# Two-layer hybrid encoder step: stage buffers laid out from both ends of on-chip memory, the last pair of each output projection reordered

## Chip, cores and metric

One core of one Trainium2 chip runs the whole kernel in one launch. The metric is device time in microseconds (us), the median of the runs. The engines are named as the profile names them: PE is TensorE's matmul and PEld its weight load, DVE is VectorE, ACT is ScalarE, POOL is GpSimd, SP is SyncE, which only issues transfers here. All operands are fp32; a matmul with fp32 precision is made of three passes over values that are split into a high and a low part.

## What is computed

A step of an encoder of two layers, width 2048, over 640 tokens (512 of a prompt, 128 of eight short samples). In each layer:

```python
h = rms_norm(x, norm_g)
z = h @ w_in                      # 2048 -> 4864 columns, in 38 blocks of 128
# a: GLU -> causal conv, width 31 -> LayerNorm -> swish -> pointwise product
# b: sliding-window attention, 16 heads;  c: attention into 256 memory rows, 4 heads
y = concatenate([y_a, y_b, y_c], -1) @ w_out   # each times its own SiLU gate
x = x + y
```

A final `rms_norm` follows the second layer. The keys, values and convolution tails are outputs as well.

## The kernel before, in words

**Layout.** Everything is kept transposed: features on the 128 partitions, the 640 tokens along the free axis. `R` holds 16 blocks of 128 features (first the residual stream x, then the attention outputs), and `HL` holds the same 16 blocks split into a high part (slots 0 to 15) and a low part (slots 16 to 31), which is what PE reads. A matmul of this kernel takes a 128x128 piece of a split weight and 320 tokens (half of them).

**Stages.** Each layer has an input stage and an output stage.

- The input stage (the loop over `ZT`, from line 907) makes one `proj` (line 737) for each of the 38 column blocks: four weight tiles of 128x512, each loaded by SP (`load`, line 147), split by ACT into `wh` (line 136) and by DVE into `wl` (line 137), and read by 24 matmuls (line 746). `wprep` (line 163) does the load and the split, out of three buffers each (`wr`, `wh`, `wl`). Convolution, attention and gates run beside it on the other engines and in between on PE.
- The output stage begins at line 1034. All 16 blocks of `R` are split into `HL` (line 1036). Output blocks j = 0 and j = 1 are plain projections with `proj` and `s_prep` (line 770), whose weights go through the buffers `sr` (raw, six of 128x768), `sh` and `sl` (two each). Beside them `combos` (line 780) forms sums and differences of the blocks of `R` and splits them into the tiles `th`/`tl` (`T[2]` to `T[4]`, 128x960 a piece, six pieces) and into `HL` itself (`T[1]`).
- The other output blocks are made two at a time by `s_pair` (line 815), a Strassen-like scheme with 7 products for 8 on 12 of the 16 input blocks. Its parts are: the product `p1` (18 matmuls); `plain` (line 835): the weights `a12` with half A of the tokens, the changed `a12` with half B (18 each), then the four other input blocks `KS` for j1 and for j2 (24 each); and the four `mixed` products `p7`, `p6`, `p4`, `p5` (18 each) with `T[3]`, `T[2]`, `T[4]`, `T[1]`. `plain` comes first; only the last pair of the second layer (`early`) has the mixed ones first.
- In the first layer all 16 output blocks are made this way; behind the last pair the next layer's `x_split` (line 877) rewrites `HL` from `R` and the first `proj` of the next input stage begins. In the second layer the pairs end at block 13; blocks 14 and 15 are made by the tail (from line 1058), which loads and splits eight weight tiles (`t_prep`), brings six blocks of the second token half back from DRAM (`y12d`, written at line 1038) and splits them into `HL`, and multiplies first 384, then 256 tokens (line 1096). The final norm and the output transfers follow.

**Buffers.** Buffers of a stage are drawn from groups that share one region of on-chip memory, one stage after the other. `phase_pools` (line 75) closes all open groups and opens the next ones from the low end: `wp` and `at` (input stage: `wr`, `wh`, `wl`, `rstd`; `at` holds what attention and convolution need), then `tt` and `sw` (output stage: the `th`/`tl` tiles; `sr`, `sh`, `sl`), then `wp` and `at` again (line 874), and at the end `tw` (line 1058: `y12`, `xr`, `xh`, `xl`). By the shapes, a partition of `wp` holds 20.5 KB, `tt` 45 KB, `sw` 30 KB and `tw` 45.5 KB. A new buffer waits for the old ones that lay in its place (`reuse_waits="tile"`).

**Order of the work.** A planner puts the instructions of each engine into one fixed order before the run, by their order in the program, with the weight preparations (`tc.high_priority`) preferred, and by a simulated timeline. All weight loads are issued by SP in program order (`load` chains them). On the chip each engine works through its list; transfers of `R`, `x1d`, `y12` and the like are issued by POOL.

## Time and profile before

| what | us |
| --- | --- |
| median of 3 runs (1858.0 to 1860.16) | 1858.42 |
| time of the profiled execution itself | 1861.93 |
| its span, first to last instruction | 1860.1 |
| PE busy | 1825.3 |
| DVE busy | 1258.2 |
| ACT busy | 789.3 |

The sums of the prediction are made in the profiled execution, whose own time is 1.83 us over its span and 3.51 us over the median. In the timeline rows below, a row gives the start in us, the busy time of the merged group, the engine, the line, the operation with the output and input tiles, and the count; in brackets stands the idle time of the engine just before and what ended it. PE's busy times contain a modelled end, so its matmuls overlap in them; distances between starts are the safer measure.

### The profile page before, as it was taken

Reading aid. Unit: us, or ns where it says so; the run is one execution under the profiler, and the core shown is the slowest. Engines: PE = TensorE matmul, PEld = TensorE weight load, DVE = VectorE, ACT = ScalarE, POOL = GpSimd, SP = SyncE. Lnnn points to the kernel's source line nnn. Section 1 sums busy time; section 2 is a strip of 40 time slices with the busy share of each in tenths; the row PEclk is TensorE's granted clock in tenths of the full one; section 3 lists DMA queues with packets and bytes.
Section 4 is the critical chain, followed back from the end, with each engine's and each line's share of the span. In section 5 each row is a group of like instructions: output and inputs, shape, how many; then the busy total and the mean of one; then the engine's idle time right before and its main releaser. Section 6 shows DMA issues by size and latency. Waiting matters only on the chain.

```text
span 1860.1 us, 32336 instructions
## 1 busy us (share of the span) xinstructions
PE 1825.3 (98%) x12612; PEld 1772.8 (95%) x12612; DVE 1258.2 (68%) x2562; ACT 789.3 (42%) x1609; POOL 160.8 (9%) x351
## 2 busy tenths in 40 slices
PE   8999999999999999999999999999999999999997
PEld 8999999999998999999999999999999999899996
DVE  7959988567555445966686999756755434776665
ACT  7831224557553334533352222555654333533331
POOL 1121110000000011100030000000000010110000
PEclk9999999999999999999999999999999999999998
DMA  8844442222222343533332332222232243452224
GB/s 280 296 116 107 104 128 76 69 65 72 87 81 74 92 154 118 186 117 114 111 108 71 81 88 79 77 66 72 65 89 81 75 131 130 128 188 75 83 79 139
DMA packets 89001, 202.30 MB, mean 109 GB/s; under 512 B 11872, under 2 KB 16912, under 8 KB 88816
## 3 DMA queue, kind: packets, MB, share of 16 engines
q1 hardware_dynamic: 68848, 139.75, 25.2%
q0 software_dynamic: 17536, 57.60, 10.0%
q10 hardware_dynamic: 2464, 2.88, 0.4%
q8 instruction: 99, 1.62, 0.4%
q14 instruction: 54, 0.44, 0.1%
HBM read 184.84 MB, written 20.33 MB: 110 GB/s over the span
## 4 chain that ended last, share of the span: by engine, by line
PE 95%; DVE 2%; DMA 1%; issue 0%; ACT 0%; DVEq 0%; ACTq 0%; POOLq 0%
PE z L746 60%; PE a L807 9%; PE z L807 8%; PE a L276 3%; PE z L299 2%; PE a L494 2%; PE a L537 2%; PE a L474 2%; PE z L1096 1%; DVE R L1129 1%; PE a L525 1%; DMA wr<-w_in 1%; PE a L633 1%; PE a L672 1%; PE a L659 1%; PE a L568 1%
## 5 line engine op out<-in xcount | busy, mean ns | idle before, releaser
L746 PE MATMUL z<-HL,wh 128*128 128x320 f32 x4864 | 950.4, 312 | 1.4 <-ACT wh L136 1.4
L746 PEld LDWEIGHTS z<-HL,wh 128*128 128x128 f32 x4864 | 768.4, 188 | 10.5 <-issue 5.7
L746 PE MATMUL z<-HL,wl 128*128 128x320 f32 x2432 | 570.4, 312 | 2.7 <-DVE wl L137 2.7
L746 PEld LDWEIGHTS z<-HL,wl 128*128 128x128 f32 x2432 | 409.4, 188 | 6.5 <-DVE wl L137 3.3
L136 ACT ACTIVATE wh<-wr 128x512 fp32r<-128x512 f32 x308 | 193.9, 630 | 472.1 <-PE z L746 384.5
L137 DVE TENSOR_TENSOR wl<-wr,wh 128x512 fp32r<-128x512 f32 x308 | 212.2, 690 | 184.6 <-ACT wh L136 172.2
L422 DVE SCALAR_TENSOR_TENSOR R<-R,sm 128x128 f32<-128x128 f32 (+1 forms) x480 | 235.3, 551 | 0.1
L136 ACT ACTIVATE sh<-sr 128x768 fp32r<-128x768 f32 (+1 forms) x133 | 103.4, 780 | 221.0 <-PE z L807 92.0
L807 PE MATMUL z<-HL,sh 128*128 128x320 f32 x728 | 160.7, 309 | 0.5 <-ACT sh L136 0.5
L137 DVE TENSOR_TENSOR sl<-sr,sh 128x768 fp32r<-128x768 f32 (+1 forms) x133 | 115.6, 871 | 41.6 <-ACT sh L136 41.6
L807 PEld LDWEIGHTS z<-HL,sh 128*128 128x128 f32 x728 | 121.7, 188 | 0.8 <-ACT sh L136 0.8
L807 PE MATMUL z<-HL,sl 128*128 128x320 f32 x364 | 113.8, 313 | 0.6 <-DVE sl L137 0.4
L807 PE MATMUL a<-th,sl 128*128 128x320 f32 x234 | 72.4, 309 | 0.8 <-DVE sl L137 0.8
L807 PE MATMUL a<-th,sh 128*128 128x320 f32 x234 | 72.3, 309 | 0.0
L807 PE MATMUL a<-tl,sh 128*128 128x320 f32 x234 | 72.3, 309 | 0.0
L807 PEld LDWEIGHTS z<-HL,sl 128*128 128x128 f32 x364 | 68.4, 188 | 3.0 <-DVE sl L137 2.9
L807 PE MATMUL a<-HL,sh 128*128 128x320 f32 x312 | 68.9, 309 | 0.0
L137 DVE TENSOR_TENSOR g<-a,g 128x512 fp32r<-128x512 f32 x80 | 49.6, 634 | 27.1 <-ACT g L136 26.5
L498 DVE CUSTOM_DVE_ANT_0 g<-a,R 128x256 f32<-128x256 f32 (+1 forms) x128 | 46.4, 388 | 23.4 <-PE a L494 20.0
L136 ACT ACTIVATE g<-a 128x512 fp32r<-128x512 f32 x80 | 42.3, 553 | 42.2 <-PE a L528 29.8
L510 ACT ACTIVATE g<-g,sml 128x256 f32<-128x256 f32 (+1 forms) x128 | 60.0, 472 | 0.0
L517 ACT ACTIVATE g<-g,sml 128x256 f32<-128x256 f32 (+1 forms) x128 | 51.5, 474 | 3.9 <-DVE sml L513 3.9
(262 smaller groups left out, 2579.0 us busy)
## 6 DMA issues: line engine op xcount, KB each, us to landing
wr<-w_in SPq DMA_DIRECT2D x304, 256.0 KB, 2.7
sr<-w_out SPq DMA_DIRECT2D x52, 384.0 KB, 3.2
sr<-w_out SPq DMA_DIRECT2D x42, 256.0 KB, 2.6
u<-w_mv SPq DMA_DIRECT2D x16, 512.0 KB, 3.5
u<-cmkT POOLq DMA_DIRECT2D x16, 512.0 KB, 4.2
u<-cmv POOLq DMA_DIRECT2D x16, 512.0 KB, 4.6
u<-w_mk SPq DMA_DIRECT2D x14, 512.0 KB, 4.3
R<-xT SPq DMA_DIRECT2D x16, 320.0 KB, 4.0
```

Of the source, the lines that this page charges most:

```text
L136: a = ac.activation(hi, raw, AF.Copy)
L137: v = ve.tensor_tensor(out=lo, in0=raw, in1=hi.bitcast(F32), op=ALU.subtract)
L276: pe.matmul(ps[ct][:, :256], w[:, ws], mslot(l, k, lo), start=k == 0 and n == 0, stop=k == NK - 1 and n == 2,)
L299: pe.matmul(psv[:, m, :], mslot(l, k, lo)[:, ms], w, start=k == 0 and n == 0, stop=k == NK - 1 and n == 2,)
L422: ve.scalar_tensor_tensor(out=o, in0=x, scalar=w, in1=o, op0=ALU.mult, op1=ALU.add)
L474: pe.matmul(ps[:, :HT], w[:, ws], x[:, k, :], start=n == 0, stop=n == 11)
L494: pe.matmul(ps[:, j, c0:256], q[:, p * P:(p + 1) * P], kk[n][h][:, (p - 1) * P + c0:(p + 1) * P], start=n == 0, stop=n == 1,)
L498: ve.tensor_tensor_reduce(out=x[:, j, c0:], in0=ps[:, j, c0:], in1=bt[:, c0:], scale=1.0, scalar=-3.0e38, op0=ALU.add, op1=ALU.max, accum_ ...
L510: ac.activation(x, x, AF.Exp, bias=ng[:, p:p + 1], accum_out=sm_[:, p:p + 1])
L517: ac.activation(x, x, AF.Copy, scale=rd[:, p:p + 1])
L746: pe.matmul(ps[:, s, :HT], w[:, ws], HL[:, lo * NK + k, s * HT:(s + 1) * HT], start=k == 0 and n == 0, stop=k == NK - 1 and n == 2,)
L807: pe.matmul(out, a[:, k * P:(k + 1) * P], b[:, k, :], start=start and k == 0 and i == 0, stop=stop and k == n - 1 and i == 2, skip_group_c ...
```

## The change

`phase_pools` is replaced by `open_pool` and `close_pool`, which open a group from the left or the right end and close one at a time. `wp` lies at the right end and `at` at the left. At the end of the input stage `at` is closed and `sw` takes its place at the left; `wp` stays open until output block j = 0, which now uses `wprep` with `wr`, `wh`, `wl`, has been written, and only then `tt` takes its place at the right. The last pair of each layer (before: of the second only) takes its mixed products first. In it the two `KS` weights are loaded ahead, then `turn(0)` closes `tt` and opens the next group at the right (`wp` in the first layer, `tw` in the second, with the read of `y12`), the `KS` products of j1 and j2 follow, then `turn(1)` (second layer: two tail weights, the split of `y12`), the result of j2, the `a12` products, `turn(2)` (the six other tail weights), and the result of j1. `sw` is closed behind that and `at` opened in its place. `xr` has two buffers where it had three.

```diff
--- before.py
+++ after.py
@@ -68,15 +68,17 @@
     dr = pool("dr", bass.MemoryType.DRAM)
 
     uid, last, cur = [0], {}, {}
-    phase = ctx.enter_context(ExitStack())
+    held_pools = {}
     home = {t: "wp" for t in ("wr", "wh", "wl", "rstd")}
     home |= {t: "at" for t in ("g2", "qh", "u5", "kc", "kh", "kl", "mh", "ml", "vh", "vl", "cqs")}
 
-    def phase_pools(*names):
-        phase.close()
-        for n in names:
-            uid[0] += 1
-            cur[n] = phase.enter_context(tc.tile_pool(name=f"{n}{uid[0]}", bufs=1, reuse_waits="tile"))
+    def open_pool(n, side):
+        uid[0] += 1
+        held_pools[n] = tc.tile_pool(name=f"{n}{uid[0]}", bufs=1, reuse_waits="tile", side=side)
+        cur[n] = held_pools[n].__enter__()
+
+    def close_pool(n):
+        held_pools.pop(n).__exit__(None, None, None)
 
     def tl(shape, tag, bufs, dt=F32, pl=None):
         uid[0] += 1
@@ -309,7 +311,8 @@
             gp.dma_start(mvd[l].rearrange("h p m d -> p h m d")[:, :, m, :], o)
 
     mraw = []
-    phase_pools("wp", "at")
+    open_pool("wp", "right")
+    open_pool("at", "left")
 
     def load_mem(j):
         if j:
@@ -812,7 +815,7 @@
     def add_to(out, ps):
         ve.tensor_tensor(out=out, in0=ps, in1=out, op=ALU.add)
 
-    def s_pair(l, j1, T, resid, early):
+    def s_pair(l, j1, T, resid, early=None):
         j2 = j1 + 1
         wj = [A["w_out"][l, j1], A["w_out"][l, j2]]
         cut = [slice(ks.start * P, ks.stop * P) for ks in (KA, KB, KS)]
@@ -832,24 +835,25 @@
         s_mm(X, p1, hl(KA, TA), True, True)
         add_to(R[:, j1, TA], X)
 
-        def plain():
-            z = pz()
+        z1 = z2 = None
+
+        def rest(z, j, start, raw=None):
+            with tc.high_priority():
+                w = s_split(raw or s_load(wj[j - j1][:, cut[2]]))
+            for s, cs in enumerate((TA, TB)):
+                s_mm(z[:, s, :HT], w, hl(KS, cs), start, True)
+
+        def plain(start):
             with tc.high_priority():
                 w = s_split(a12)
-            s_mm(z[:, 0, :HT], w, hl(KB, TA), True, False)
+            s_mm(z1[:, 0, :HT], w, hl(KB, TA), start, not start)
             with tc.high_priority():
                 sub(a12, a12, s2)
                 w = s_split(a12)
-            s_mm(z[:, 1, :HT], w, hl(KB, TB), True, False)
-            w = s_prep(wj[0][:, cut[2]])
-            for s, cs in enumerate((TA, TB)):
-                s_mm(z[:, s, :HT], w, hl(KS, cs), False, True)
-            add_to(half(R[:, j1, :]), z[:, :, :HT])
-            z = pz()
-            w = s_prep(wj[1][:, cut[2]])
-            for s, cs in enumerate((TA, TB)):
-                s_mm(z[:, s, :HT], w, hl(KS, cs), True, True)
-            add_to(half(R[:, j2, :]), z[:, :, :HT])
+            s_mm(z1[:, 1, :HT], w, hl(KB, TB), start, not start)
+
+        def into(j, z):
+            add_to(half(R[:, j, :]), z[:, :, :HT])
 
         def mixed(raw, n, out, start, dst):
             with tc.high_priority():
@@ -862,16 +866,36 @@
         p7 = (a21, 3, Dd, True, [(j2, TB)])
         p5 = (s1, 1, X, False, [(j2, TB), (j1, TB)])
         p4 = (a22, 4, Dd, False, [(j2, TA)])
-        if not early:
-            plain()
-        for a in (p7, p6, p4, p5):
-            mixed(*a)
+        order = (p7, p6, p4, p5)
         if early:
-            plain()
+            for a in order:
+                mixed(*a)
+            with tc.high_priority():
+                st = [s_load(w[:, cut[2]]) for w in wj]
+            early(0)
+            z1, z2 = pz(), pz()
+            rest(z1, j1, True, st[0])
+            rest(z2, j2, True, st[1])
+            early(1)
+            into(j2, z2)
+            plain(False)
+            early(2)
+            into(j1, z1)
+        else:
+            z1 = pz()
+            plain(True)
+            rest(z1, j1, False)
+            into(j1, z1)
+            z2 = pz()
+            rest(z2, j2, True)
+            into(j2, z2)
+            for a in order:
+                mixed(*a)
 
     for l in range(L):
         if l:
-            phase_pools("wp", "at")
+            close_pool("sw")
+            open_pool("at", "left")
         cur["rstd"] = rstd = tl([P, TOK], "rstd", 1)
         for k in range(0 if l else 8, NK):
             x_split(l, k)
@@ -1031,7 +1055,8 @@
                     push(samples.pop(0))
             step(7 if bg and bg[0] is not lnt else 2)
 
-        phase_pools("tt", "sw")
+        close_pool("at")
+        open_pool("sw", "left")
         for k in range(NK):
             split(R[:, k, :], None, HL[:, k, :], HL[:, NK + k, :])
         if l == L - 1:
@@ -1039,15 +1064,49 @@
         acc = w25()
         resid = A["xT"] if l == 0 else x1d
         done = NK if l == 0 else NK - 2
-        T = None
+        T, W = None, []
+
+        def t_prep(src):
+            with tc.high_priority():
+                raw = tl([P, 512], "xr", 2, F32, cur["tw"])
+                load(raw, src)
+                hi = tl([P, 512], "xh", 8, F32R, cur["tw"])
+                lo = tl([P, 512], "xl", 8, F32R, cur["tw"])
+                split(raw, None, hi, lo)
+                return hi, lo
+
+        def turn(step):
+            if step == 0:
+                close_pool("tt")
+                open_pool("tw" if l == L - 1 else "wp", "right")
+            if l < L - 1:
+                return
+            if step == 0:
+                cur["y12"] = tl([P, 6, HT], "y12", 1, F32, cur["tw"])
+                with tc.high_priority():
+                    gp.dma_start(cur["y12"], y12d)
+                return
+            for p in (range(2), range(2, 8))[step - 1]:
+                W.append(t_prep(A["w_out"][l, NK - 2 + p // 4][:, p % 4 * 512:(p % 4 + 1) * 512]))
+            if step == 1:
+                b12 = hl(KA, TB)
+                for g in (0, 3):
+                    ks = slice(g, g + 3)
+                    split(cur["y12"][:, ks, :], None, b12[0][:, ks, :], b12[1][:, ks, :])
+
         for j in list(range(2)) + list(range(2, done, 2)):
             if j < 2:
                 res = zt()
                 gp.dma_start(res, resid[j])
-                ps = proj([A["w_out"][l, j][:, c * 512:(c + 1) * 512] for c in range(4)], s_prep)
+                ps = proj(
+                    [A["w_out"][l, j][:, c * 512:(c + 1) * 512] for c in range(4)], s_prep if j else wprep
+                )
                 ve.tensor_tensor(out=half(R[:, j, :]), in0=ps[:, :, :HT], in1=half(res), op=ALU.add)
             else:
-                s_pair(l, j, T, resid, l == L - 1 and j + 2 == done)
+                s_pair(l, j, T, resid, turn if j + 2 == done else None)
+            if j == 0:
+                close_pool("wp")
+                open_pool("tt", "right")
             if j == 1:
                 T = combos()
             for i in range(j, j + 1 if j < 2 else j + 2):
@@ -1055,27 +1114,6 @@
                     gp.dma_start(x1d[i], R[:, i, :])
                 add_sq(i, i == 0, acc)
 
-    phase_pools("tw")
-
-    def t_prep(src):
-        with tc.high_priority():
-            raw = tl([P, 512], "xr", 3, F32, cur["tw"])
-            load(raw, src)
-            hi = tl([P, 512], "xh", 8, F32R, cur["tw"])
-            lo = tl([P, 512], "xl", 8, F32R, cur["tw"])
-            split(raw, None, hi, lo)
-            return hi, lo
-
-    y12 = tl([P, 6, HT], "y12", 1, F32, cur["tw"])
-    with tc.high_priority():
-        gp.dma_start(y12, y12d)
-        b12 = hl(KA, TB)
-        for g in (0, 3):
-            ks = slice(g, g + 3)
-            split(y12[:, ks, :], None, b12[0][:, ks, :], b12[1][:, ks, :])
-    W = [
-        t_prep(A["w_out"][L - 1, NK - 2 + p // 4][:, p % 4 * 512:(p % 4 + 1) * 512]) for p in range(8)
-    ]
     res = [zt(), zt()]
     for j in range(2):
         gp.dma_start(res[j], x1d[NK - 2 + j])
@@ -1134,6 +1172,8 @@
                 (sy if k % 4 == 1 else ac).dma_start(
                     A["yT"][k - 1:k + 1, :, cs].rearrange("k p n -> p k n"), R[:, k - 1:k + 1, cs]
                 )
+    close_pool("tw")
+    close_pool("sw")
 
 
 _OUT = {
```

## Rows read from the trace of the kernel before

**Rows 1.** What PE waited for over the whole span: engine, line, tile, the releaser, then us in total, times, longest us. 12 such rows make up 24.4 us; one of them.

```profile
PE z L1096 <- ACT xh L136: 2.3, 1, 2.3
```

**Rows 2.** The chain of waits, merged: start us, us, engine, tile, line, count. A stretch of the second layer's input stage and the last stretch of its last pair, both without a gap.

```profile
1120.44 30.07 PE z L746 x205
...
1796.63 12.33 PE z L807 x84
```

**Rows 3.** Timeline around the end of the first layer's input stage and the first weights of its output stage.

```profile
746.64 51.02 SPq L147 DMA_DIRECT2D sr<-w_out  x16
...
752.38 0.46 PE L746 MATMUL z<-HL,wl 128*128 128x320 f32 x2
...
753.26 1.14 ACT L136 ACTIVATE sh<-sr 128x512 fp32r<-128x512 f32 x2
...
753.93 0.86 PE L746 MATMUL z<-HL,sh 128*128 128x320 f32 x4 [1.10 <-ACT sh L136]
...
755.71 0.56 PE L746 MATMUL z<-HL,sl 128*128 128x320 f32 x2 [0.92 <-DVE sl L137]
```

**Rows 4.** The same place of the second layer.

```profile
1618.43 0.46 PE L746 MATMUL z<-HL,wl 128*128 128x320 f32 x2
...
1619.98 0.86 PE L746 MATMUL z<-HL,sh 128*128 128x320 f32 x4 [1.10 <-ACT sh L136]
...
1621.76 0.56 PE L746 MATMUL z<-HL,sl 128*128 128x320 f32 x2 [0.92 <-DVE sl L137]
```

**Rows 5.** Timeline 20 us later in the second layer, at the second weight tile of output block j = 1.

```profile
1632.41 2.23 DVE L775 TENSOR_TENSOR R<-R 128x960 f32<-128x960 f32 x2 [2.77 <-DMA y12d<-R]
...
1638.89 0.75 PE L746 MATMUL z<-HL,sh 128*128 128x320 f32 x4
...
1641.22 0.69 DVE L137 TENSOR_TENSOR sl<-sr,sh 128x512 fp32r<-128x512 f32 x1
...
1641.97 0.90 PE L746 MATMUL z<-HL,sl 128*128 128x320 f32 x2 [2.33 <-DVE sl L137]
...
1645.24 0.45 PE L746 MATMUL z<-HL,sl 128*128 128x320 f32 x2
```

**Rows 6.** Timeline of the turn from the first layer's last pair to the second layer's first projection (weights issued at 959.76).

```profile
959.76 34.72 SPq L147 DMA_DIRECT2D wr<-w_in  x12
...
962.85 3.00 ACT L139 ACTIVATE HL<-R,sm 128x640 fp32r<-128x640 f32 x4 [2.38 <-PE a L807]
...
964.70 0.31 PE L807 MATMUL a<-HL,sl 128*128 128x320 f32 x1
...
965.75 1.66 ACT L136 ACTIVATE wh<-wr 128x512 fp32r<-128x512 f32 x3
...
966.42 0.86 PE L746 MATMUL z<-HL,wh 128*128 128x320 f32 x4 [1.41 <-ACT wh L136]
...
968.44 0.56 PE L746 MATMUL z<-HL,wl 128*128 128x320 f32 x2 [1.16 <-DVE wl L137]
...
973.02 0.75 PE L746 MATMUL z<-HL,wh 128*128 128x320 f32 x4
```

**Rows 7.** Timeline of the turn from the second layer's last pair to the tail.

```profile
1791.23 26.31 SPq L147 DMA_DIRECT2D xr<-w_out  x8
...
1808.64 0.31 PE L807 MATMUL z<-HL,sl 128*128 128x320 f32 x1
...
1809.90 0.74 ACT L252 ACTIVATE w<-R 128x640 f32<-128x640 f32 x1 [2.83 <-DVE R L813]
1810.54 1.14 ACT L136 ACTIVATE xh<-xr 128x512 fp32r<-128x512 f32 x2
...
1811.21 0.62 PE L1096 MATMUL z<-HL,xh 128*128 128x384 f32 x2 [2.26 <-ACT xh L136]
...
1812.15 0.52 PE L1096 MATMUL z<-HL,xl 128*128 128x384 f32 x1 [0.32 <-DVE xl L137]
...
1815.90 0.34 PE L1096 MATMUL z<-HL,xl 128*128 128x384 f32 x1
```

**Rows 8.** Stretches of the span: us, then PE, PEld, DVE, ACT and POOL busy us (instructions), the granted TensorE clock as a share of full speed, DMA share, GB/s.

```profile
768.00:795.00 27.00, 26.85 (x184) 26.59 (x183) 20.96 (x26) 11.68 (x15) 7.47 (x14) 1.00 0.70 239
...
1640.00:1661.00 21.00, 18.07 (x110) 17.55 (x111) 19.51 (x23) 8.98 (x12) 6.39 (x12) 0.92 0.65 219
```

**Rows 9.** DVE's groups by shape, in 753 to 800 us and in 940 to 990 us: busy us, mean ns of one, idle before.

```profile
L137 DVE TENSOR_TENSOR tl<-R,th 128x960 fp32r<-128x960 f32 x6 | 7.0, 1160 | 0.0
...
L140 DVE SCALAR_TENSOR_TENSOR HL<-R,sm,HL 128x640 fp32r<-128x640 f32 x16 | 13.5, 882 | 1.9 <-ACT HL L139 1.9
```

**Rows 10.** Small gaps of PE inside pairs: the first layer's last pair, and the second layer's first pair.

```profile
957.12 0.41 PE L807 MATMUL a<-th,sl 128*128 128x320 f32 x1 [0.79 <-DVE sl L137]
...
1659.43 0.56 PE L807 MATMUL z<-HL,sh 128*128 128x320 f32 x2 [0.53 <-ACT sh L136]
...
1660.42 0.42 PE L807 MATMUL z<-HL,sl 128*128 128x320 f32 x1 [0.44 <-DVE sl L137]
```

**Rows 11.** Transfers issued from 1785 to 1820 us: count, KB each, median us from issue to landing.

```profile
xr<-w_out SPq DMA_DIRECT2D x8, 256.0 KB, 3.1
y<-y12d POOLq DMA_DIRECT2D x1, 960.0 KB, 7.5
```

**Rows 12.** The same columns as rows 8, for the instructions on the tile `tl` alone.

```profile
753.00:768.00 15.00, 0.00 (x0) 0.00 (x0) 3.26 (x3) 1.00 0.40 124
```

## Prediction, made before the changed kernel was run

> **What bounds the kernel now.** PE does. In the table above PE is busy for 1825.3 of a span of 1860.1 us, so 34.8 us are all that an unchanged set of 12,612 matmuls could give back. I read the views in this order: the list of what PE waited for [rows 1], the chain of waits for stretches without a gap [rows 2], then the timeline wherever the chain leaves PE. A matmul on 320 tokens costs 30.07/205 = 0.147 us in such a stretch [rows 2]; one on 384 tokens 0.147 x 384/320 = 0.176. With these I measure each gap from start to start, since PE's ends are modelled: the distance to the next start, less the matmuls in between at full rate.
>
> - First weights of the output stage, first layer [rows 3]. Two matmuls start at 752.38, so the next is due at 752.67; it starts at 753.93 (1.26 late). Four run, the next is due at 754.52 and starts at 755.71 (1.19). Loss 2.45 us. The load had been issued at 746.64, but ACT splits the weight only at 753.26, and PE waits for just that.
> - The same place in the second layer [rows 4]: 1618.72 to 1619.98 and 1620.57 to 1621.76, again 2.45 us.
> - Second layer, block j = 1 [rows 5]: due at 1639.48, started at 1641.97, 2.49 late. Then 12 matmuls take 3.27 us up to 1645.24 instead of 1.76, part of them at the lower level of the clock, whose grant is 0.92 over this stretch [rows 8]: 1.51 more. Loss 4.00. DVE had stood 2.77 us for the write of `y12d` and did the weight's low part late.
> - Turn between the layers [rows 6]: due at 964.85, started 966.42 (1.57); four matmuls, due 967.01, started 968.44 (1.43); then 20 matmuls take 4.58 us up to 973.02 instead of 2.93 (1.65, the clock). Loss 4.65 us. The weights were issued at 959.76, yet ACT splits them at 965.75, behind four `HL` splits that waited for the pair's last product.
> - Turn to the tail [rows 7]: due 1808.79, started 1811.21 (2.42); two matmuls, due 1811.56, started 1812.15 (0.59); then 12 up to 1815.90 take 3.75 instead of 2.11 (1.64). Loss 4.65. The weights had been issued at 1791.23; ACT splits them at 1810.54, behind a square that had waited for the pair's result.
> - Small ones inside pairs [rows 10]: 0.79 in the last pair of layer one, 0.53 + 0.44 in the first pair of layer two.
>
> All this is 20.0 us, and in none of it does PE wait for a weight's transfer. What is late is the place of the first weight split in ACT's fixed order. My reading is that the planner counts a group as free only when all old groups under it are: `sw` waits for the last use of `at`, `tw` (45.5 KB, reaching 0.5 KB beyond `tt`) for the end of `sw`, hence of the whole pair.
>
> **The change, part by part.** No matmul, split or byte is added or taken; everything is order and place.
>
> 1. *j = 0 on `wprep`.* Its four weights use the running ring `wr`, which waits for nothing but itself, so they are split like those of any input projection, where 205 matmuls run in a row [rows 2]. This takes away 2.45 us in each layer, 4.90. On SP's queue the four loads pass ahead of j = 1's, which still wait for `at`; that wait ended at 746.64 before [rows 3], and j = 1 starts 96 x 0.147 = 14.1 us after 752.67, at 766.8, so 20 us cover it. The next thing due is `HL` of the last gate block, wanted by the last six of those 96 matmuls, 13 us on.
> 2. *`tt` opens only after j = 0.* The six `tl` splits (1.16 us each [rows 9]) may now start only at 766.8; three, 3.26 us of DVE, were before 768 until now [rows 12]. DVE has 27 - 20.96 = 6.0 us idle from 768 to 795 [rows 8], and `p7` needs `T[3]` only some 13 us into the first pair, behind `p1` and most of `plain`. So I cost it at nothing in layer one. If that cover goes, the small gaps of the first pair grow. In layer two DVE has only 21 - 19.51 = 1.5 us idle from 1640 to 1661 [rows 8]: bounds 0 and 3.26 - 1.5 = 1.8 us. I take 1.0 per layer, nearer the two gaps of 0.97 that this backlog made before [rows 10].
> 3. *j = 1 in layer two.* The `y12d` write and DVE's wait for it stay. But j = 0 no longer uses `sh`/`sl`, so j = 1's first two weights find both buffers empty and can be split before DVE stops. The bounds are 0 and 4.00 gained; I take 3.5, since the weight that came too late is one of those two.
> 4. *Turn between the layers.* `tt` is given up at the end of `p4`, and 18 (`p5`) + 84 matmuls follow, 15.0 us at 0.147 (84 took 12.33 [rows 2]). The `w_in` loads, their splits and `HL` blocks 0 to 3 (free after the `KS` products, 36 matmuls or 5.3 us ahead) fit in, so the 4.65 should go. What is moved against it: 10 of the 16 `HL` blocks stay locked until the `KS` and `a12` products instead of 6, so four more splits of 0.88 us [rows 9], 3.5 us of DVE, fall into the turn; the projection wants one block in 6 x 0.147 = 0.88 us, just DVE's pace. Bounds 0 and 3.5; I take 1.0, like the gap of 0.79 that such splits already made [rows 10]. That gap itself may go, as the mixed products leave the end: 0.8 gained, or none; I take 0.5. The result of j2 is added ahead of the `a12` products, so the accumulator for the next projection is free.
> 5. *Turn to the tail.* Two of eight tail weights and the `y12` split (two DVE pieces of about 1.16 us) move ahead of the `a12` products, with 5.3 us to spare. The read of `y12` takes 7.5 us on POOL's queue [rows 11]; 15.0 us are left for it, and POOL has nothing urgent behind. With two `xr` buffers a weight pair turns round in about 3.1 us [rows 11] plus a split of 0.6 and 0.7, 4.4, against 2 x 12 x 0.176 = 4.2 us of PE work: 0.2 us late at each of the two last pairs at worst, less the lead. The 4.65 should go; I take off 0.5 (bounds 0 and 2).
>
> Sum: 4.90 + 3.5 + 4.65 + 0.5 + 4.65 - 2.0 - 1.0 - 0.5 = 14.7 us off. The best case is all 20.0. The profiled execution's own 1861.93 becomes 1847.2; it stood 3.51 over the median of the runs, so the median 1858.42 becomes **1843.7**.
>
> **The rivals.**
>
> - *The first pairs get crowded* (chance 0.12). The `T` splits meet the pair's weight splits on DVE, PE waits 1.8 us more in layer two, the clock falls (1.6 [rows 6, 7]), and j = 1's 4.00 stay. For it: DVE's 1.5 us of idle time. Against: `T` is wanted late. 14.7 - 3.5 - 1.8 - 1.6 = 7.8 off: 1850.6.
> - *The turn starves on `HL`* (0.12). The four extra splits stand ahead of the block that PE wants: 3.5 us and a slow stretch of 1.65 instead of my 1.0. 14.7 - 4.2 = 10.5 off: 1847.9.
> - *It doesn't do what it says* (0.08). The next stage's splits stay behind the pair's end in ACT's order, because the planner counts otherwise than I read. Then only j = 0's 4.90 is gained: 1853.5. For it: at the tail the raw weights had lain ready long before the split [rows 7].
> - *Slower* (0.05). ACT gets the six `T` splits ahead of j = 1's weights. They wait for the last matmul of j = 0, and the weights behind them wait too: six pieces of 1.0 us, then 0.6 + 0.7 for the weight, 7.3 us, and 1.65 of slow clock, 9.0 per layer. Against 14.2 (4.90 + 4.65 + 4.65) gained, 18.0 lost gives 3.8 slower: 1862.2. It decides from about 7 us per layer. The mechanism is there already: weight splits at 965.75 behind four `HL` splits [rows 6]. Against it: the weight splits have priority, and two of them have empty buffers 12 us before. [...]
>
> **How the numbers follow.** A measurement of this kernel can tell about 0.2%, 3.7 us, from no change. My own case has 0.63, at 1843.7, between 1838.4 (all 20.0) and 1847.9 (the 14.2 of 1, 4 and 5, less half of the bounds 3.5, 2 and 1.8). The range to 1852 takes in the first two rivals; outside lie the third, the slower one and the edges. Faster by over 0.2%: my case, the first two rivals and a third of the doubtful 1853.5, about 0.89; the rest of that rival and two others at once make 0.06 within 0.2%; slower 0.05.
>
> **What would show it.** Right: no gap of PE over 0.5 us between the last gate projection and j = 0 in either layer; the first `wh` split of layer two and the first `xh` split of the tail ahead of their pair's last matmul; PE's granted clock at 1.00 in the stretches of [rows 8] and at both turns; PE's waits down from 24.4 to about 10 us. Wrong: `th` or `tl` among what ACT or DVE holds while PE waits for `sl`; PE waiting for `HL` in layer two's first projection; a first split still behind the squares.

## The result and the profile after

The changed kernel takes **1848.32 us** (median of 4 runs, 1847.06 to 1848.58), the kernel before beside it 1859.13 (4 runs): ratio 0.9941, 95% interval 0.9923 to 0.9958, 10.8 us less. The forecast was 14.7 less. Run once more, unaltered (e5 below), it stood at 0.9935 (0.9922 to 0.9949).

The page of the changed kernel, first its span, then busy time by engine. PE's work is the same 12,612 matmuls.

```profile
span 1846.7 us, 32347 instructions
...
PE 1817.5 (98%) x12612; PEld 1766.3 (96%) x12612; DVE 1257.8 (68%) x2562; ACT 786.6 (43%) x1609; POOL 160.7 (9%) x351
```

What PE waited for over the span (compare [rows 1]): releaser, us in total, times, longest.

```profile
PE z L810 <- ACT sh L138: 2.9, 4, 1.4
...
PE z L810 <- DVE sl L139: 2.1, 3, 1.5
PE z L749 <- DVE sl L139: 2.1, 2, 1.7
```

All its waits make 18.2 us, where it was 24.4. `ACT sh` in z L746, `ACT wh`, `ACT xh` and `DVE xl` are gone from the list; waits for `sh` and `sl` inside the pairs (L810) are new or longer.

The chain of waits, merged (start, us, engine, tile, line, count): the first projection of the output stage in layer one, the turn between the layers, layer two's j = 0, and the turn to the tail.

```profile
749.61 16.15 PE z L749 x110
...
960.93 1.18 PE z L749 x8
...
964.16 2.35 PE z L810 x16
...
1610.71 5.30 PE z L749 x36
...
1797.60 4.95 PE z L1134 x28
...
1803.73 2.35 PE z L810 x16
```

Where [rows 3, 4, 6, 7] had gaps of 2.45, 2.45, 4.65 and 4.65, PE now runs from one stage into the next. At the turns there is more to it than was forecast: the fixed order has 20 matmuls of the projection (line 749) and 33 of the tail (line 1134) ahead of the pair's last 16 (line 810). The two timelines of ACT show why at the turns: the next stage's first splits stand ahead of the last splits of the running pair.

```profile
951.23 0.62 ACT L138 ACTIVATE wh<-wr 128x512 fp32r<-128x512 f32 x1
...
953.90 0.84 ACT L138 ACTIVATE sh<-sr 128x768 fp32r<-128x768 f32 x1 [0.49 <-PE z L810]
...
1785.71 0.62 ACT L138 ACTIVATE xh<-xr 128x512 fp32r<-128x512 f32 x1
...
1797.41 0.85 ACT L138 ACTIVATE sh<-sr 128x768 fp32r<-128x768 f32 x1
```

PE's first matmuls of the projection and of the tail start at 960.77 and 1797.44, so the first splits began 9.5 and 11.7 us ahead of them; before, PE waited 1.41 and 2.26 for them [rows 6, 7].

**New gaps in layer one** (timeline of DVE, then of ACT and PE). The result of j = 0 is added at 765.78, and the six `tl` pieces follow; the low part of j = 1's third weight, whose high part ACT had ready at 769.8, stands behind five of them.

```profile
765.78 0.82 DVE L1104 TENSOR_TENSOR R<-z,zt 128x640 f32<-128x640 f32 x1 [1.04 <-PE z L749]
...
767.59 2.22 DVE L139 TENSOR_TENSOR tl<-R,th 128x960 fp32r<-128x960 f32 x2
...
770.79 3.29 DVE L139 TENSOR_TENSOR tl<-R,th 128x960 fp32r<-128x960 f32 x3
774.00 0.69 DVE L139 TENSOR_TENSOR sl<-sr,sh 128x512 fp32r<-128x512 f32 x1
```

```profile
769.16 0.62 ACT L138 ACTIVATE sh<-sr 128x512 fp32r<-128x512 f32 x1
...
774.74 0.56 PE L749 MATMUL z<-HL,sl 128*128 128x320 f32 x2 [1.66 <-DVE sl L139]
```

PE, counted from start to start as in the prediction, is 1.82 us late there; 0.32, 0.84 and 0.43 follow in the first pair, of which the last two are all but absent (0.2 together) in the other profile of this same kernel, e5.

**New gaps in layer two** (timeline of DVE, then of PE). DVE stops for the write of `y12d`, 3.17 us where it was 2.77 [rows 5], has the six `tl` pieces behind it, two of them ahead of the third weight, and passes the delay on to the first pair.

```profile
1625.63 2.23 DVE L778 TENSOR_TENSOR R<-R 128x960 f32<-128x960 f32 x2 [3.17 <-DMA y12d<-R]
```

```profile
1634.60 0.56 PE L749 MATMUL z<-HL,sl 128*128 128x320 f32 x2 [0.42 <-DVE sl L139]
...
1642.25 0.56 PE L810 MATMUL z<-HL,sh 128*128 128x320 f32 x2 [0.35 <-ACT sh L138]
...
1646.69 0.41 PE L810 MATMUL z<-HL,sl 128*128 128x320 f32 x1 [1.53 <-DVE sl L139]
...
1650.71 0.56 PE L810 MATMUL z<-HL,sh 128*128 128x320 f32 x2 [1.41 <-ACT sh L138]
...
1651.71 0.41 PE L810 MATMUL z<-HL,sl 128*128 128x320 f32 x1 [0.44 <-DVE sl L139]
```

From start to start these are 0.58 (and 0.18 behind it) at j = 1, then 0.51, 1.69, 1.56 and 0.71 in the first pair.

Stretches (us; then PE, PEld, DVE, ACT, POOL busy us and instructions, granted clock, DMA share, GB/s). The first and the third are those of [rows 8].

```profile
768.00:795.00 27.00, 24.34 (x161) 23.29 (x160) 20.36 (x24) 10.49 (x14) 6.90 (x13) 1.00 0.61 205
...
770.00:780.00 10.00, 8.34 (x57) 8.07 (x57) 9.96 (x12) 3.50 (x4) 3.19 (x6) 1.00 0.56 191
...
1640.00:1661.00 21.00, 17.28 (x112) 16.23 (x112) 13.65 (x17) 5.34 (x8) 5.83 (x11) 1.00 0.68 240
```

The reader is to compare the first two: over 27 us DVE looks as idle as before, yet for the 10 us around the third weight it has nothing free.

**Where the time came from.** By start-to-start gaps the places that the change touches lost 20.8 us before (the 20.0 of the prediction, with its three small ones counted this way, and 0.31 in layer one's first pair) and lose 9.3 after: 1.82 + 1.59 + 0.66 in layer one (0.66 is in its last pair) and 0.76 + 4.47 in layer two. That is 11.5, against 10.8 between the medians. The two profiled executions, from which the gaps are read, differ by 13.4 (1861.93 and 1848.52); 1.5 of that lies ahead of the first changed place, where the 5,150th matmul starts at 750.10 and 748.64, and belongs to the executions.

**What the sums of gaps leave out.** Behind a gap the granted clock of PE sometimes fell: in the kernel before, behind its gap at layer two's j = 1, it was 0.50 in each half microsecond from 1642.0 to 1645.0, and 1.00 from 1645.5 on. The same gaps cost it in one execution and not in another. In e5, this same kernel, it is 0.87 over 1652 to 1665 (the 12 matmuls from 1651.96 to 1655.16 start 0.267 us apart, where 0.147 is usual), and the first pair of layer two takes some 1.5 us longer than in e1 below, which has the same gaps there and 1.00.

### The profile page after: what moved, and what is told of

It is laid out like the page before. It is cut to its first block, busy times and chain, and to the rows that moved or that the text cites. A ratio compares the mean times of both kernels' runs of the same rounds, so it can differ in the third digit from the quotient of the medians.

```text
span 1846.7 us, 32347 instructions
## 1 busy us (share of the span) xinstructions
PE 1817.5 (98%) x12612; PEld 1766.3 (96%) x12612; DVE 1257.8 (68%) x2562; ACT 786.6 (43%) x1609; POOL 160.7 (9%) x351
## 4 chain that ended last, share of the span: by engine, by line
PE 94%; DVE 3%; DMA 1%; issue 0%; ACT 0%; DVEq 0%; ACTq 0%
PE z L749 59%; PE a L810 9%; PE z L810 9%; PE z L301 2%; PE a L278 2%; PE a L497 2%; PE a L540 2%; PE a L477 2%; PE z L1134 1%; DVE R L1167 1%; PE a L528 1%; DMA wr<-w_in 1%; PE a L636 1%; PE a L675 1%; PE a L662 1%; PE a L571 1%
## 5 line engine op out<-in xcount | busy, mean ns | idle before, releaser
L749 PE MATMUL z<-HL,wh 128*128 128x320 f32 x4992 | 973.8, 312 | 0.0
L749 PEld LDWEIGHTS z<-HL,wh 128*128 128x128 f32 x4992 | 787.8, 188 | 8.9 <-issue 5.6
L749 PE MATMUL z<-HL,wl 128*128 128x320 f32 x2496 | 584.1, 312 | 1.0 <-DVE wl L139 1.0
L749 PEld LDWEIGHTS z<-HL,wl 128*128 128x128 f32 x2496 | 419.6, 188 | 4.5 <-issue 1.6
L138 ACT ACTIVATE wh<-wr 128x512 fp32r<-128x512 f32 x316 | 198.6, 629 | 467.4 <-PE z L749 383.9
L139 DVE TENSOR_TENSOR wl<-wr,wh 128x512 fp32r<-128x512 f32 x316 | 217.7, 689 | 177.8 <-ACT wh L138 165.4
L138 ACT ACTIVATE sh<-sr 128x768 fp32r<-128x768 f32 (+1 forms) x125 | 98.2, 788 | 203.3 <-PE z L810 92.4
L810 PE MATMUL z<-HL,sh 128*128 128x320 f32 x728 | 161.1, 309 | 2.9 <-ACT sh L138 2.9
L139 DVE TENSOR_TENSOR sl<-sr,sh 128x768 fp32r<-128x768 f32 (+1 forms) x125 | 110.0, 882 | 38.7 <-ACT sh L138 38.5
L810 PEld LDWEIGHTS z<-HL,sh 128*128 128x128 f32 x728 | 121.6, 188 | 4.0 <-ACT sh L138 4.0
L810 PE MATMUL z<-HL,sl 128*128 128x320 f32 x364 | 113.6, 312 | 2.3 <-DVE sl L139 2.1
L810 PEld LDWEIGHTS z<-HL,sl 128*128 128x128 f32 x364 | 68.3, 188 | 4.9 <-DVE sl L139 4.9
L810 PE MATMUL a<-th,sh 128*128 128x320 f32 x234 | 72.2, 308 | 0.0
L810 PE MATMUL a<-th,sl 128*128 128x320 f32 x234 | 72.2, 308 | 0.0
L810 PE MATMUL a<-tl,sh 128*128 128x320 f32 x234 | 72.2, 308 | 0.0
L810 PE MATMUL a<-HL,sh 128*128 128x320 f32 x312 | 68.9, 308 | 0.0
L513 ACT ACTIVATE g<-g,sml 128x256 f32<-128x256 f32 (+1 forms) x128 | 59.7, 468 | 0.0
L816 DVE TENSOR_TENSOR R<-a,R 128x320 f32<-128x320 f32 x78 | 37.1, 489 | 25.3 <-PE a L810 24.8
```

Source lines behind the costliest of these rows:

```text
L138: a = ac.activation(hi, raw, AF.Copy)
L139: v = ve.tensor_tensor(out=lo, in0=raw, in1=hi.bitcast(F32), op=ALU.subtract)
L513: ac.activation(x, x, AF.Exp, bias=ng[:, p:p + 1], accum_out=sm_[:, p:p + 1])
L749: pe.matmul(ps[:, s, :HT], w[:, ws], HL[:, lo * NK + k, s * HT:(s + 1) * HT], start=k == 0 and n == 0, stop=k == NK - 1 and n == 2,)
L810: pe.matmul(out, a[:, k * P:(k + 1) * P], b[:, k, :], start=start and k == 0 and i == 0, stop=stop and k == n - 1 and i == 2, skip_group_c ...
L816: ve.tensor_tensor(out=out, in0=ps, in1=out, op=ALU.add)
```

## The experiments

Two theories of the missing 4 us. **Order (place):** `tl` pieces that wait for j = 0's memory stand ahead of urgent weight splits in DVE's fixed list; put them elsewhere and the gaps go. **Pace:** between j = 0's result and the first pair DVE has no time to spare; whatever comes first, something is late.

**e1: the free place first.** Which of the three `T` tiles lies where.

```
-            for n in (2, 3, 4)
...
-        T[2], T[3], T[4] = tt
+            for n in (3, 2, 4)
...
+        T[3], T[2], T[4] = tt
```

> The changed kernel with the six th/tl tiles laid out in the order T[3], T[2], T[4] instead of T[2], T[3], T[4], so that both pieces of T[3] and one of T[2] lie beside wp and not in its place. Theory (place): the gaps of PE at j = 1 and in the first pairs of the changed kernel (1.82 + 1.59 us in layer one, 0.76 + 4.47 in layer two, 8.6 in all) come from tl splits that may not start before j = 0 gives up wp; with two of the six free earlier, 2.3 us of DVE work leave the crowded stretch in each layer and the gaps fall to about 5: 1845, between 1843.5 and 1847. Rival (pace): PE simply runs through j = 0 without its old gap of 2.45 us, so DVE has that much less time before the first pair, wherever the tiles lie: no change, 1848.3 within 1.

Measured: 1848.06 us, ratio 0.9927 (0.9915 to 0.9940). The place theory missed, its rival's time came. DVE's list is unchanged, all six `tl` pieces still come behind j = 0's result, and the gap at j = 1 is 1.83. Where a tile lies in the new group doesn't matter for the order of the list; the planner seems to count the closed group as a whole, as the prediction read it.

**e2: the head as before.** Steps 1 and 2 undone: j = 0 on `s_prep`, `tt` opened at once.

```
+        close_pool("wp")
+        open_pool("tt", "right")
...
-  s_prep if j else wprep
+  s_prep
...
-            if j == 0:
-                close_pool("wp")
-                open_pool("tt", "right")
```

> The changed kernel with its first part undone: wp is closed and tt opened as soon as the output stage begins, and j = 0 takes its weights through sr, sh, sl as before; the two-ended layout and the reordered last pairs stay. Theory (place): the first-weight gaps return (2.45 in each layer) and the late weight of j = 1 in layer two (4.00), while the crowding goes back to 0.4 and 1.4: 1848.3 + 4.9 + 3.2 - 6.1 = 1850.3, between 1849 and 1852; both turns stay without a gap. Rival (pace) expects the same time here. If part one were worth its full 4.9 + 3.5 without a price: 1856.7.

Measured: 1851.04 us, ratio 0.9939 (0.9925 to 0.9953), as expected. The head's gaps are back (PE's timeline; 2.49 by starts in layer one, 1.26 in layer two and 1.19 behind it) and the backlog's are gone. At layer two's j = 1 it loses 1.25 and 0.90, where the kernel before lost 2.49 and a slow stretch.

```profile
753.95 1.27 PE L749 MATMUL z<-HL,sh 128*128 128x320 f32 x4 [2.33 <-ACT sh L138]
...
1615.47 0.86 PE L749 MATMUL z<-HL,sh 128*128 128x320 f32 x4 [1.09 <-ACT sh L138]
```

By the ratios to the kernel before, this can't be told from the changed kernel, so most of the gain is the two turns. Beside e1, which has the changed kernel's order and ran on the same chip, it is 3.0 us slower (five runs each, 1849.5 to 1851.77 and 1847.61 to 1849.53). Gaps are the smaller part of that, 8.7 in all against 8.0; the granted clock is 0.86 over 750 to 762 and 0.87 over 1615 to 1628 here, and 1.00 in e1 (over the whole span 0.994 here, 0.997 there). So steps 1 and 2 together bring some 3 us at most, and part of it through the clock.

**e3: the turns as before.** Plain products where they were (first in layer one, last in layer two), the next stage's loads behind the pair; layout and j = 0 as changed.

```
         if early:
+            if l < L - 1:
+                plains()
             for a in order:
                 mixed(*a)
-            with tc.high_priority():
-                st = [s_load(w[:, cut[2]]) for w in wj]
-            early(0)
...
-            early(2)
-            into(j1, z1)
+            if l == L - 1:
+                plains()
...
+        for step_ in range(3):
+            turn(step_)
```

> The changed kernel with the last pairs in their old order and the next stage's buffers opened only behind them; j = 0 on wprep and the two-ended layout stay. Both theories: the two turns cost what they did before, 4.65 each, so 1848.3 + 9.3 = 1857.6, between 1856 and 1859. If the layout from two ends alone frees the next stage's first splits, the turns stay closed: 1848 to 1850.

Measured: 1853.77 us, ratio 0.9956 (0.9944 to 0.9969). Half a miss, and a useful one. The turn between the layers has the gaps of [rows 6] again (PE, late by 1.55 and 1.44), without the slow stretch behind them:

```profile
965.46 0.85 PE L749 MATMUL z<-HL,wh 128*128 128x320 f32 x4 [1.40 <-ACT wh L138]
967.49 0.56 PE L749 MATMUL z<-HL,wl 128*128 128x320 f32 x2 [1.17 <-DVE wl L139]
```

but the turn to the tail stays closed. Two `xh` splits stand ahead of the pair's last `sh` split, at 1798.80, on ACT:

```profile
1797.76 1.14 ACT L138 ACTIVATE xh<-xr 128x512 fp32r<-128x512 f32 x2
1798.80 0.62 ACT L138 ACTIVATE sh<-sr 128x512 fp32r<-128x512 f32 x1
```

So the layer turn's gain comes from the order, the tail's from the layout alone. That it is because `tw`, with one `xr` buffer less and from the right end, no longer reaches into `sw`, is my reading; it wasn't tested apart.

**e4: hold `T` twice as long.** j = 1 too on `wprep`, `wp` closed behind it.

```
-  s_prep if j else wprep
+  wprep
...
-            if j == 0:
+            if j == 1:
                 close_pool("wp")
```

> The changed kernel with j = 1 on wprep as well and wp given up only after j = 1, so that the T splits that lie in wp's place are held back by another 14.1 us. Theory (place): the gap at j = 1 goes (1.8), but 7 us of tl splits now meet the first pair's own splits, and PE waits some 3 us more there in each layer: 1852, between 1849 and 1856. Rival (pace): the hold is not what PE waits for, only the gaps at j = 1 go: 1846.

Measured: 1856.31 us, ratio 0.9969 (0.9957 to 0.9980), just over the upper end. The gap at j = 1 is gone, and the first pair loses 0.96 + 4.03 in layer one and 1.40 + 4.03 in layer two. Timeline of DVE, then PE:

```profile
786.77 4.36 DVE L139 TENSOR_TENSOR tl<-R,th 128x960 fp32r<-128x960 f32 x4
```

```profile
793.86 0.63 PE L810 MATMUL z<-HL,sl 128*128 128x320 f32 x1 [3.76 <-DVE sl L139]
```

The same places lose 7.3 us in e1, 3.1 less, but the time is 8.2 over e1's, beside which it ran. Most of the rest is the clock: 0.74 over 787 to 800 and over 1652 to 1665, where e1 has 1.00. The later `T` may start, the more PE loses: that much is shown.

**e5: the changed kernel once more**, beside e6 to e8.

> The changed kernel once more, unaltered, beside the other three on one chip: 0.994 of the kernel before, with the gaps of its first profile.

Measured: 1849.59 us, ratio 0.9935 (0.9922 to 0.9949); gaps 1.82 and 0.31 in layer one, 0.69 (and 0.17 behind it), 0.52, 1.68, 1.57, 0.70 in layer two.

**e6: a group of its own for `T[3]`** and the high part of `T[2]`, beside `sw`, free from the start.

```
-  tl([P, 6, HT], f"th{n}", 1, F32R, cur["tt"])
+  tl([P, 6, HT], f"t{w}{n}", 1, F32R, cur["t3" if n == 3 or (w, n) == ("h", 2) else "tt"])
...
         open_pool("sw", "left")
+        open_pool("t3", "left")
```

> The changed kernel with T[3] and one piece of T[2] in a group of their own (t3) at the left beside sw, opened when at is closed, where nothing of wp lies; the rest of T stays in tt, opened after j = 0. e1_t3_clear moved the tiles and left DVE's order as it was, all six tl splits behind the result of j = 0. Theory (planner counts a group as a whole): with a group of its own the two tl3 splits come ahead of j = 0's result, 2.3 us of DVE leave the crowd, and the 1.82 at j = 1 of layer one falls to under 0.5; some 2 to 3 us less than the changed kernel in all. Theory (pace): the order changes and the gaps move on to the next weight: less than 1 us gained.

Measured: 1847.67 us, ratio 0.9928 (0.9915 to 0.9940), not to be told from e5. In layer one a single `tl` piece now stands ahead of j = 0's result, where two were expected, and three instead of five between it and the third weight. The gap at j = 1 falls from 1.82 to 0.86, but 1.07 + 0.70 turn up in the first pair. In layer two no piece came forward, and only the gap at j = 1 changed (0.36 for 0.69). This speaks for pace.

**e7: write `y12d` in two halves**, so that the first half starts before the last three blocks are ready.

```
-            gp.dma_start(y12d, R[:, KA, TB])
+            for g in (0, 3):
+                gp.dma_start(y12d[:, g:g + 3, :], R[:, KA.start + g:KA.start + g + 3, TB])
```

> The changed kernel with the write of y12d in two transfers of three blocks each, so that the first differences of combos need only the first, which can start as soon as block 12 is gated. Theory (layer two is crowded by DVE's stop of 3.2 us for that write): the stop shrinks to under 1.5 us and layer two's gaps at j = 1 and in the first pair, 5.2 us in all, fall to about 2: 2 to 4 us less than the changed kernel. Rival (the hold of the T splits alone makes them): no change in layer two's gaps.

Measured: **1843.3 us, ratio 0.9905 (0.9891 to 0.9918)**, the fastest of all. The first half is issued some 9 us ahead of the second (POOL), and DVE does three subtractions without a stop where it waited 3.17:

```profile
1608.86 0.78 POOL L1064 DMA_DIRECT2D y12d<-R  x1 [9.62 <-DVE R L715]
...
1618.22 0.76 POOL L1064 DMA_DIRECT2D y12d<-R  x1 [1.94 <-DVE R L1050]
```

```profile
1619.64 3.41 DVE L778 TENSOR_TENSOR R<-R 128x960 f32<-128x960 f32 x3
```

Layer two's gaps fall from 5.3 (e5) to 2.14 and have layer one's form, 1.82 at j = 1 and 0.32. The medians differ by 6.3, the two profiled executions by 7.4. Of these 7.4, 3.2 are the gaps; 2.5 lie ahead of the edit (the third weight of layer one's j = 1 at 772.90 here, at 775.36 there) and belong to the executions; 1.7 are left, most of it the clock behind the gaps of layer two's first pair, 1.00 here over 1652 to 1665 and 0.87 in e5, where it cost some 1.5.

**e8: e6 and e7 together.**

> Both edits, the group of its own for T[3] and the write of y12d in two. If the two causes add, 4 to 6 us less than the changed kernel, 0.991 of the kernel before; layer two's first pair keeps its old gap of 1.4 at most.

Measured: 1845.25 us, ratio 0.9914 (0.9902 to 0.9927): no better than e7. In both layers 0.85 at j = 1 and 1.06 + 0.70 in the first pair.

**e9: `T` behind the third weight.**

```
-        split(raw, None, hi, lo)
+        held_s.append(split(raw, None, hi, lo))
...
-        T = {}
+        T, gate = {}, held_s[-2]
...
-                split(R[:, ab[i], cs], None, T[n][0][:, ks, :], T[n][1][:, ks, :])
+                with tc.issue_after(gate[0]) if n in (2, 4, 1) else nullcontext():
+                    with tc.issue_after(gate[1]) if n in (2, 4, 1) else nullcontext():
+                        split(R[:, ab[i], cs], None, T[n][0][:, ks, :], T[n][1][:, ks, :])
```

> The changed kernel, with one edit: the splits of T[2], T[4] and HL's T[1] are recorded behind the split of j = 1's third weight (in the changed kernel five of the six tl pieces stand ahead of that split on DVE, and PE waits 1.82 us for it in layer one). 'Order' theory: DVE takes its list strictly in order, so with two tl pieces ahead instead of five the low part of the third weight is there 3 x 1.1 = 3.3 us earlier and the 1.82 at j = 1 of layer one goes to 0; layer two, where DVE's stop for the y12d write decides, keeps its 5.2. That is 1.8 us under the changed kernel: ratio to the kernel before 0.9925 (the unaltered changed kernel stood at 0.9935). 'Pace' theory: DVE has too little spare time between the result of j = 0 and the first pair, whatever the order; then the 1.82 turns up again as 1 to 2 us in the first pair (p1, or the combined products that need T), and the ratio stays at 0.9935.

Measured: 1848.65 us, ratio 0.9933 (0.9920 to 0.9946). The order did what it was to do, and it brought nothing: the 1.82 is gone, 1.27 + 0.71 stand in the first pair instead.

**e10: e9's edit with e7's.**

> The same edit, and the y12d write in two transfers of three blocks. With the write in two alone, PE's gaps were 1.82 at j = 1 and 0.32 in the first pair in each layer. 'Order' theory: 1.82 goes in both layers, 3.6 us under that kernel: ratio 0.9886, some 1839.5 us where the write in two alone had 1843.3. 'Pace' theory: the gaps move into the first pairs (1 to 2 us each), ratio 0.9900 to 0.9910 like the kernel that combined the write in two with T[3] in a place of its own (0.9914).

Measured: 1844.75 us, ratio 0.9911 (0.9897 to 0.9924), with 1.26 + 0.71 in the first pair of each layer. Timelines of layer one, DVE, ACT, then PE:

```profile
771.41 0.69 DVE L139 TENSOR_TENSOR sl<-sr,sh 128x512 fp32r<-128x512 f32 x1
...
785.24 0.96 DVE L780 TENSOR_TENSOR sr<-sr,sr 128x768 f32<-128x768 f32 x1
```

```profile
786.31 1.36 ACT L138 ACTIVATE sh<-sr 128x768 fp32r<-128x768 f32 x2 [3.09 <-DVE sr L780]
```

```profile
787.20 0.56 PE L814 MATMUL z<-HL,sh 128*128 128x320 f32 x2 [1.11 <-ACT sh L138]
788.20 0.42 PE L814 MATMUL z<-HL,sl 128*128 128x320 f32 x1 [0.43 <-DVE sl L139]
```

The third weight's low part begins 5.0 us behind the addition of j = 0 (766.40 here) instead of 8.2, but DVE works without a stop from 766.40 to 786.2; the combination of a raw weight at 785.24 is the last thing in that row, ACT's split waits for it, PE for the split. ACT waits 3.09 for that combination and not for a free buffer, so the rival that the two `sh`/`sl` buffers set the pace isn't what the rows show.

**e11: e7 again**, beside e9 and e10.

> The write of y12d in two transfers alone, on the chip of the two kernels above, so that their ratios can be set beside it: 0.9905 again (0.989 to 0.992), gaps 1.82 at j = 1 and 0.32 in the first pair in each layer by either theory.

Measured: 1844.8 us, ratio 0.9913 (0.9901 to 0.9926). Its median equals e10's: moving the `T` pieces is worth nothing, with e9 the second time. Its profile has 2.43 at layer one's j = 1 where 1.82 was expected (0.31 in the first pair, and 1.83 and 0.31 in layer two), and behind it a clock of 0.83 over 770 to 780.

**e12: less work for DVE.** e10, with three combinations of raw weights of each first pair on GpSimd.

```
-            ve.tensor_tensor(out=s1, in0=a21, in1=a22, op=ALU.add)
-            sub(s2, s1, a11)
-            sub(a21, a11, a21)
+            cb = gp if j1 == 2 else ve
+            cb.tensor_tensor(out=s1, in0=a21, in1=a22, op=ALU.add)
+            cb.tensor_tensor(out=s2, in0=s1, in1=a11, op=ALU.subtract)
+            cb.tensor_tensor(out=a21, in0=a11, in1=a21, op=ALU.subtract)
```

> The kernel with T[2], T[4] and T[1] behind the third weight and the y12d write in two (its ratio was 0.9911), with one edit more: of the first pair of each layer three combinations of raw weights (s1, s2 and a21, 0.95 us each on DVE) are made by GpSimd, which is busy for 9% of the span. 'Pace' theory: in that kernel DVE has no idle time from the result of j = 0 to the first pair, and the gaps (1.26 + 0.71 in the first pair of each layer) came from the combination of a12 (started at 785.24) and the split behind it; 2.85 us off DVE bring that combination forward by about as much, both gaps fall under 0.5 in each layer, some 3 us less: ratio 0.9895. Other theory: the two sh/sl buffers set the pace, not DVE's work; then the gaps stay at 1 to 2 us per layer and the ratio at 0.9911.

Measured: 1855.6 us, ratio 0.9968 (0.9956 to 0.9981), the other way than either theory had it. Timelines of GpSimd, DVE and PE in layer one:

```profile
772.59 6.50 POOL L837 TENSOR_TENSOR sr<-sr,sr 128x768 f32<-128x768 f32 x1 [4.12 <-DVE sl L139]
779.16 2.44 POOL L839 TENSOR_TENSOR sr<-sr,sr 128x768 f32<-128x768 f32 x1
```

```profile
777.65 2.24 DVE L139 TENSOR_TENSOR sl<-sr,sh 128x768 fp32r<-128x768 f32 x1 [0.27 <-ACT sh L138]
779.82 2.80 DVE L139 TENSOR_TENSOR HL<-R,HL 128x960 fp32r<-128x960 f32 x1
...
783.27 2.06 DVE L139 TENSOR_TENSOR sl<-sr,sh 128x768 fp32r<-128x768 f32 x1
...
789.09 0.94 DVE L780 TENSOR_TENSOR sr<-sr,sr 128x768 f32<-128x768 f32 x1
```

```profile
785.38 0.42 PE L814 MATMUL z<-HL,sl 128*128 128x320 f32 x1 [1.57 <-DVE sl L139]
...
791.05 0.56 PE L814 MATMUL z<-HL,sh 128*128 128x320 f32 x2 [3.05 <-ACT sh L138]
```

Beside GpSimd a DVE piece of 0.95 takes 2.24 and one of 1.16 takes 2.80; four such (at 777.65, 779.82, 783.27 and 785.25) raise DVE's work by 5.7 us where 2.85 were taken off. DVE comes to the combination of `a12` 22.3 us behind the addition of j = 0 (789.09 less 766.80) instead of 18.8 in e10 (785.24 less 766.40), 3.5 later, and PE's gaps in the first pair grow from 1.97 to 5.64 (1.73, 3.21 and 0.70), by 3.7. Meant to relieve DVE, the run loaded it, and PE lost about what DVE was later: that is pace, seen from the other side. The clock added to it, 0.87 over 787 to 800 and 0.74 over 1652 to 1665, where e10 has 1.00. Pace is shown where DVE loses a stop (e7) and where it gets more to do (e12); what less work for DVE would gain of the last 2 us per layer was not shown.

## Why the prediction was right, and where its sum was off

The time lies inside the range, but nearer to the first rival's 1850.6 than to my own 1843.7: the mechanisms of steps 1, 3, 4 and 5 came in the main as described, and step 2 cost three times its term. Each step by its start-to-start gaps, layer one and layer two together:

| step | forecast | measured |
|---|---|---|
| 1, j = 0 on `wprep` | 4.90 | 4.90 |
| 2, `tt` opened after j = 0 | -2.0 | -6.2 |
| 3, j = 1 of layer two | 3.5 | 3.2 |
| 4, turn between layers and last pair | 4.15 | 4.9 |
| 5, turn to the tail | 4.15 | 4.65 |
| sum | 14.7 | 11.5 |

- **Step 1** held in both layers: no gap between the last gate projection and j = 0.
- **Step 3** held in size: 4.00 became 0.76. The reason given (two empty buffers ahead of DVE's stop) moved the wait to the third weight, 0.58. With j = 0 back on `sh` and `sl`, e2 has gaps of 2.15 there again, which bears the reason out.
- **Step 4** held and was better: no wait for `HL`, so the 1.0 set against it was not lost (the pair's last 16 matmuls, which run behind the projection's first 20, give the `HL` splits time; that is a reading, not tested); the 0.94 in the last pair became 0.66, half of what was hoped. e3 confirms that the order makes it.
- **Step 5** held in size, with a reason too many. The weights needed not be moved ahead of the `a12` products; the layout alone does it (e3). That fits the prediction's reading of the 0.5 KB by which `tw` reached into `sw`.
- **Step 2 failed**, as a term that was mis-sized. "I cost it at nothing in layer one" and "I take 1.0 per layer", with an upper bound of 1.8, against 3.1 in each layer (1.82 + 1.59 - 0.31, and 4.47 - 1.39; 1.8 in layer one in the second profile). The mistake is in the cover. Of DVE's 6.0 us of idle time in 768 to 795 [rows 8], 4.66 stood just ahead of 794.96 (the kernel before, below), behind the deadline and not ahead of it. The deadline was taken to be `T[3]`, 13 us into the first pair; it is the next `sl` in DVE's list, the third weight, wanted at 772.9. From 765.78 until then are 7.1 us, and DVE's list had 8.2 ahead of it, the sum of j = 0 (0.74 from start to start), two subtractions and five `tl` pieces (1.07 each); with the split itself, 0.7, that is the 1.8. In layer two the write of `y12d` took 3.17 more out of the same stretch, and e7 gives 3.2 back.

```profile
794.96 0.69 DVE L137 TENSOR_TENSOR sl<-sr,sh 128x512 fp32r<-128x512 f32 x1 [4.66 <-ACT sh L136]
```

- **The rivals.** The first one, crowded first pairs, had the mechanism and was put at 0.12 as if it excluded my own case. It came beside it, in both layers and at j = 1 already. The stated sign of it, `tl` held by DVE while PE waits for `sl`, is what the rows show; its two other terms, a slow clock and the 4.00 of j = 1, did not come in this profile. The `HL` rival and the one in which nothing is done did not come. The slower one did not come either: ACT did wait 3.66 us for j = 0's last product with `th` at the head of its list (765.83), but DVE had split j = 1's first two weights at 754.11 and 754.71.
- **The clock** was 1.00 in both stretches of [rows 8], as said; in e5 it was 0.92 in the second. PE's waits were to fall to about 10 and fell to 18.2, for step 2's reason.

What stays open: the 0.84 + 0.43 in layer one's first pair, there in one profile of this kernel and not in the other; and the last 2 us per layer, which neither order nor place (e1, e6, e8 to e10) gives back.

A version that beats both kernels is e7: the changed kernel with the `y12d` write in two, 0.9905 (0.9891 to 0.9918) and once more 0.9913 (0.9901 to 0.9926).

## What to carry to other kernels

When a step holds work back, add up what its engine's list has between the release and the next thing that anyone waits for in that same list, and set it against the time to that deadline; idle time averaged over a longer stretch covers nothing. Here, reordering a full list only moved the gap (1.82 at j = 1 became 1.27 + 0.71 in the first pair, e9); a stop of 3.17 us taken out of it (one transfer made two, e7) came back whole, 3.2.

## What the hardware showed beyond expectation

- DVE and GpSimd held each other up. GpSimd's first sum ended at 779.09 (772.59 + 6.50), and the DVE piece that started at 777.65 ended at 779.89, 0.8 us behind it; the next one ended at 782.62, 1.0 behind GpSimd's second (781.60). That reads as if each of the two had waited for GpSimd's sum and then taken about its usual 0.95 or 1.16; the profile counts all of it as busy. The other way round, the first sum took 6.50 where the next took 2.44: DVE worked without a stop until 777.38, and the sum ended 1.7 behind that, as the second ended 1.7 behind the DVE piece at 779.89. What makes the two hold each other up these rows do not show. The DVE piece at 783.27 doesn't fit so simply: it took 2.06, and the profile has only transfer issues of GpSimd beside it until 784.77, which cost DVE nothing in e10 (0.95 for the same piece at 782.17, beside the issues from 781.82 on). That stays open.
- The same gaps did not always cost clock. With 1.27 + 0.71 in e9 the granted clock was 0.76 in the 7 us around and behind the gaps; with 1.26 + 0.71 in e10 it stayed at 1.00 (stretches of e9, then of e10). What tells the two apart was not found.

```profile
786.00:793.00 7.00, 6.02 (x29) 5.76 (x29) 1.78 (x3) 1.65 (x3) 0.00 (x0) 0.76 0.78 297
```

```profile
786.00:793.00 7.00, 5.46 (x36) 5.10 (x36) 1.75 (x3) 1.82 (x3) 0.08 (x1) 1.00 0.93 362
```
